# Multi-query attention: the transposes of q, k and the outputs go from TensorE to DMA transposes

## Chip, cores, metric

One core of a Trainium2 chip. The metric is the device time of one execution in microseconds (us). Engines: PE (TensorE: matmuls and transposes), PEld (its weight loads), DVE (VectorE), ACT (ScalarE), POOL (GpSimd), SP (SyncE, which here only issues DMAs). PSUM is the memory into which the code has PE write, SBUF holds all other tiles on the chip.

## The reference

```python
# q: [8, 1024, 16, 64]; k, v: [8, 1024, 64]: all 16 heads share one k and one v
scores = np.matmul(q, k.transpose(0, 1, 3, 2)) / np.sqrt(head_dim)
weights = np.exp(scores - np.max(scores, axis=-1, keepdims=True))
weights = weights / np.sum(weights, axis=-1, keepdims=True)
attn_out = np.matmul(weights, v)
```

## The kernel before

Work goes by *pairs* of heads: 8 batches x 8 pairs = 64. A *window* `w` computes the scores and exponentials of pair `w` while PE sums and multiplies with v for pair `w - 1`. A window has 8 *cycles* (`cy`), each with two *units* of 128x1024 scores. Of a window's 16 units ACT exponentiates 14; units 2 and 8, so in cycles 1 and 4, go to DVE, which does it in seven instructions (`z`, then `f, t, g, t, g, wt`). PE, ACT and DVE run their instructions in the order in which the program emits them.

```python
scp = ctx.enter_context(tc.tile_pool(name="scp", bufs=3, space=PSUM))  # scores: three buffers
b1p = ctx.enter_context(tc.tile_pool(name="b1p", bufs=2, space=PSUM))  # accumulators AND transposes
DVE_UNITS = (2, 8)
# ... (cut)
def trans_q(p):                     # 8 PE transposes, then a DVE copy
    s, r = divmod(p, 2)
    qps = b1p.tile([P, S], FP16, tag="b1", name=f"qps{p}")
    for c in range(NKT):
        nc.tensor.transpose(qps[:, c * P : (c + 1) * P], qn[s][:, c, r * P : (r + 1) * P], ident16)
    qt[p] = qtp.tile([P, S], FP16, tag="qt", name=f"qt{p}")
    nc.vector.tensor_copy(out=qt[p], in_=qps)
# ... (cut)
for w in range(NP + 2):
    a = w - 1
    for cy in range(NCY):
        unit(w, 2 * cy); unit(w, 2 * cy + 1)          # scores, exponential
        for i in range(3 * cy, 3 * cy + 3):
            av_slot(a, i)                             # sums (ones) and products with v
        if cy == 3 and w > 0: trans_q(w + 1)          # 8 transposes + copy
        if cy == 4: sums(a)                           # 4 small transposes + reciprocal
        if cy == 6: finish(a, 0)                      # 4 transposes + multiply
        if cy == 1: finish(w - 2, 1)                  # 4 transposes + multiply + store
        # ... (cut: conditions; k transposed in cycle 7 of the window before a new batch)
        for _ in range(4):
            if late: late.pop(0)()                    # DVE's steps of the exponential
```

The softmax here doesn't subtract the row's maximum and nothing guards it: scores larger than these inputs give would overflow.

## Time and profile before

926.04 us (median of 4 runs, 925.94 to 926.36).

| | before |
|---|---|
| span of the profiled run | 924.2 us |
| ACT busy | 848.8 us (92%) |
| PE busy | 813.3 us (88%) |
| DVE busy | 790.4 us (86%) |
| ACT idle before its exponentials | 62.3 us, 10.7 of it the start |
| pace in steady state | 13.91 us a window |

In the groups of instructions the columns are: line, engine, operation, output<-input tiles and shapes, count | busy us, mean ns of one | idle us of the engine just before them <-what it waited for. Four groups of the kernel before:

```profile
L146 ACT ACTIVATE wt<-sc 128x1024 f16<-128x1024 f32 x896 | 847.5, 1030 | 62.3 <-PE sc L134 54.6
L150 DVE TENSOR_SCALAR z<-sc 128x1024 uint16<-128x1024 f32 x128 | 156.1, 1219 | 60.9 <-PE sc L134 60.9
L222 PE MATMUL tr<-ident,ots 128*128 128x128 f16 x512 | 50.8, 222 | 24.0 <-DVE ots L202 24.0
L123 PE MATMUL qps<-ident,qn 128*128 128x128 f16 x512 | 39.7, 221 | 27.0 <-DVE ots L202 23.2
```

Everybody waits a little: ACT and DVE for PE's scores, PE's transposes for DVE's evictions. Next, ACT alone in order of time in the kernel before (start us, length us, engine, line, operation, shapes, count, idle before and releaser): first three lines from window 0 (the last two of the 13 are window 1's), then lines from steady state.

```profile
12.75 1.94 ACT L146 ACTIVATE wt<-sc 128x1024 f16<-128x1024 f32 x2 [10.73 <-PE sc L134]
15.53 1.02 ACT L146 ACTIVATE wt<-sc 128x1024 f16<-128x1024 f32 x1 [0.84 <-PE sc L134]
17.05 12.02 ACT L146 ACTIVATE wt<-sc 128x1024 f16<-128x1024 f32 x13 [0.49 <-PE sc L134]
...
64.87 11.41 ACT L146 ACTIVATE wt<-sc 128x1024 f16<-128x1024 f32 x12
76.45 1.02 ACT L146 ACTIVATE wt<-sc 128x1024 f16<-128x1024 f32 x1 [0.16 <-PE sc L134]
77.86 12.34 ACT L146 ACTIVATE wt<-sc 128x1024 f16<-128x1024 f32 x13 [0.39 <-PE sc L134]
90.36 1.02 ACT L146 ACTIVATE wt<-sc 128x1024 f16<-128x1024 f32 x1 [0.16 <-PE sc L134]
```

### The profile page before, as it was taken

The numbers are of one execution on the slowest core, as the hardware profiler recorded it, in microseconds if no ns is written. First come the engines' busy times: TensorE is split into PE (matmuls) and PEld (weight loads), VectorE is DVE, ScalarE is ACT, GpSimd is POOL, SyncE is SP. The second block draws the span as 40 slices with busy tenths as digits, with TensorE's granted clock in tenths as the row PEclk, the third lists the DMA queues.
The fourth block names the chain that finished last, engine by engine and source line by source line (L and its number), as shares of the span: only waits on it lengthen the run. The fifth ranks groups of instructions, "written<-read, shape, count | busy, mean of one in ns | idle before, by whom it ended". The sixth has DMA issues, their size and how long they took to land.

```text
span 924.2 us, 18181 instructions
## 1 busy us (share of the span) xinstructions
PE 813.3 (88%) x7488; PEld 291.1 (31%) x7488; DVE 790.4 (86%) x1371; ACT 848.8 (92%) x897; POOL 36.0 (4%) x46
## 2 busy tenths in 40 slices
PE   4998889988898889889899898999898898898986
PEld 1233333333333333333333333333333333333332
DVE  4798898898888898888988988888888889889886
ACT  4999999999999999999999999999999999999994
POOL 3000000000000000000000000000000000000000
PEclk9899999999999999999999999999999999999999
DMA  9033332233232243322342313432314323101102
GB/s 159 4 67 69 58 70 52 47 69 80 49 67 52 47 80 61 61 50 49 76 75 47 69 49 56 75 69 48 65 39 64 70 54 61 47 24 46 47 24 69
DMA packets 116563, 54.64 MB, mean 59 GB/s; under 512 B 18176, under 2 KB 116480, under 8 KB 116480
## 3 DMA queue, kind: packets, MB, share of 16 engines
q0 software_dynamic: 41600, 17.83, 16.3%
q1 hardware_dynamic: 74880, 35.66, 13.7%
q8 instruction: 58, 0.95, 0.4%
q14 instruction: 25, 0.20, 0.1%
HBM read 37.75 MB, written 33.55 MB: 77 GB/s over the span
## 4 chain that ended last, share of the span: by engine, by line
DVE 46%; ACT 27%; PE 20%; issue 6%; DMA 1%; POOL 0%; DVEq 0%; ACTq 0%; POOLq 0%
ACT wt L146 27%; DVE z L150 8%; PE acc L188 6%; PE sc L134 6%; DVE osb L223 5%; DVE ots L202 5%; DVE t L169 5%; DVE wt L175 5%; DVE g L172 5%; PE acc L196 4%; DVE qt L127 4%; DVE t L159 3%; DVE f L156 3%; DVE g L164 3%; PE tr L222 3%
## 5 line engine op out<-in xcount | busy, mean ns | idle before, releaser
L146 ACT ACTIVATE wt<-sc 128x1024 f16<-128x1024 f32 x896 | 847.5, 1030 | 62.3 <-PE sc L134 54.6
L134 PE MATMUL sc<-qt,k2t 64*128 64x512 f16 x2048 | 328.3, 386 | 26.0 <-ACT wt L146 23.0
L196 PE MATMUL acc<-wt,v 128*64 128x512 f16 x2048 | 305.5, 389 | 11.1 <-DVE rec L212 10.9
L150 DVE TENSOR_SCALAR z<-sc 128x1024 uint16<-128x1024 f32 x128 | 156.1, 1219 | 60.9 <-PE sc L134 60.9
L196 PEld LDWEIGHTS <-v 128*64 128x64 f16 x2048 | 90.1, 108 | 199.0 <-issue 172.2
L188 PE MATMUL acc<-wt,ones 128*32 128x512 f16 x2048 | 146.9, 386 | 0.4 <-DVE osb L223 0.3
L134 PEld LDWEIGHTS <-k2t 64*128 64x128 f16 x2048 | 80.9, 94 | 177.3 <-issue 150.4
L202 DVE CAST ots<-acc 128x512 f16<-128x512 f32 x192 | 130.9, 682 | 0.4 <-PE acc L188 0.2
L223 DVE TENSOR_TENSOR osb<-tr,rec 128x512 f32<-128x512 f16 x128 | 88.0, 687 | 36.9 <-PE tr L222 36.0
L175 DVE TENSOR_TENSOR wt<-z,g 128x1024 uint16<-128x1024 uint16 x128 | 88.6, 692 | 13.8 <-ACT wt L146 0.5
L169 DVE TENSOR_TENSOR t<-f,t 128x1024 f16<-128x1024 uint16 x128 | 87.5, 684 | 0.0
L172 DVE TENSOR_TENSOR g<-t,g 128x1024 f16<-128x1024 f16 x128 | 87.1, 680 | 0.1
L222 PE MATMUL tr<-ident,ots 128*128 128x128 f16 x512 | 50.8, 222 | 24.0 <-DVE ots L202 24.0
L123 PE MATMUL qps<-ident,qn 128*128 128x128 f16 x512 | 39.7, 221 | 27.0 <-DVE ots L202 23.2
L188 PEld LDWEIGHTS <-ones 128*32 128x32 f16 x2048 | 37.4, 95 | 73.0 <-issue 58.9
L159 DVE TENSOR_SCALAR t<-f 128x1024 f16<-128x1024 uint16 x128 | 54.7, 427 | 4.4
L112 POOL DMA_DIRECT2D qn<-in_q_dram x32 | 28.2, 882 | 707.4 <-PE qps L123 624.6
L222 PEld LDWEIGHTS <-ots 128*128 128x128 f16 x512 | 28.9, 97 | 81.9 <-DVE ots L202 55.1
L164 DVE TENSOR_SCALAR g<-f 128x1024 f16<-128x1024 uint16 x128 | 53.7, 420 | 0.0
L156 DVE TENSOR_SCALAR f<-z 128x1024 uint16<-128x1024 uint16 x128 | 51.3, 401 | 0.1
L123 PEld LDWEIGHTS <-qn 128*128 128x128 f16 x512 | 34.1, 98 | 51.8 <-issue 47.8
L127 DVE COPY qt<-qps 128x1024 f16<-128x1024 f16 x64 | 43.7, 683 | 5.9 <-PE qps L123 5.9
(18 smaller groups left out, 78.3 us busy)
## 6 DMA issues: line engine op xcount, KB each, us to landing
out_dram<-osb SPq DMA_DIRECT2D x64, 512.0 KB, 3.2
qn<-in_q_dram POOLq DMA_DIRECT2D x32, 512.0 KB, 5.6
kn<-in_k_dram SPq DMA_DIRECT2D x8, 256.0 KB, 3.3
v<-in_v_dram POOLq DMA_DIRECT2D x8, 128.0 KB, 3.5
```

What stands on the lines that cost most here:

```text
L134: nc.tensor.matmul(sc[:, h, :], k2t[64 * h : 64 * h + 64, j * P : (j + 1) * P], qt[p][64 * h : 64 * h + 64, c * QC : (c + 1) * QC], start= ...
L146: nc.scalar.activation(out=w, in_=sc, func=EXP, scale=ascale)
L150: nc.vector.tensor_scalar(out=z, in0=sc, scalar1=15 * ONE, scalar2=None, op0=ALU.add)
L159: nc.vector.tensor_scalar(out=t, in0=f, scalar1=-ONE, scalar2=1.0 / ONE, op0=ALU.add, op1=ALU.mult)
L169: nc.vector.tensor_tensor(out=t, in0=f, in1=t, op=ALU.mult)
L172: nc.vector.tensor_tensor(out=g, in0=t, in1=g, op=ALU.mult)
L175: nc.vector.tensor_tensor(out=w.bitcast(U16), in0=z, in1=g, op=ALU.add)
L188: nc.tensor.matmul(a[32 * g : 32 * g + 32, :], ones16, w[:, h, cq * QC : (cq + 1) * QC], start=(j == 0), stop=(j == NKT - 1), tile_positio ...
L196: nc.tensor.matmul(a[64 * h : 64 * h + 64, :], vt[:, j, :], w[:, h, cq * QC : (cq + 1) * QC], start=(j == 0), stop=(j == NKT - 1), tile_po ...
L202: nc.vector.tensor_copy(out=o, in_=a)
L222: nc.tensor.transpose(tr[:, i, :], ots[p, cq + 1][:, i * P : (i + 1) * P], ident16)
L223: nc.vector.tensor_tensor(out=osb[p][:, 4 * cq : 4 * cq + 4, :].rearrange("p i (h d) -> p (i h) d", h=2), in0=tr.rearrange("p i (h d) -> p ...
```

## The change

The intent: take transposes off PE, the copies behind them off DVE, and both out of the PSUM buffers shared with the accumulators. q, k (from the second batch on) and the outputs with their sums are transposed by DMA, from SBUF to SBUF. The first pair's q and the last pair's output stay on PE.

```diff
     def trans_k(b):
+        if b > 0:
+            st["k2t"] = kvp.tile([P, S], FP16, tag="k2t", name=f"k2t{b}")
+            nc.sync.dma_start_transpose(...)          # cut
+            return
 ...
-        qn[s] = qp.tile([P, NKT, 4 * D], FP16, ...)   # a q load of 4 heads every second window
+        qn[p] = qp.tile([P, NKT, 2 * D], FP16, ...)   # of 2 heads every window
 ...
     def trans_q(p):
+        # cut: p == 0 as before
+        qt[p] = qtp.tile([P, NKT, P], FP16, tag="qt", name=f"qt{p}")
+        nc.sync.dma_start_transpose(out=qt[p], in_=qn[p].rearrange("p c x -> p (c x)"))
 ...
+    def turn(p):
+        otq[p] = otqp.tile([P, 12, P], FP16, tag="otq", name=f"otq{p}")
+        nc.sync.dma_start_transpose(out=otq[p], in_=ots[p].rearrange("p g x -> p (g x)"))
+
+    def finish(p):       # reciprocal and ONE multiply of 128x1024, from SBUF; then the store
 ...
+            load_q(w + 3)
+            trans_q(w + 2)
-                    if cy == 3 and w > 0: trans_q(w + 1)
-                    if cy == 4: sums(a)
-                    if cy == 6: finish(a, 0)
-                if cy == 1 and 0 <= w - 2 < NP: finish(w - 2, 1)
+                    if cy == NCY - 1: turn(a)         # cut: the last pair on PE
+                if cy == 5 and 0 <= w - 2 < NP - 1: finish(w - 2)
```

More of the change, by code (lines that the diff above doesn't have):

```diff
@@ L52 @@
     otsp = ctx.enter_context(tc.tile_pool(name="otsp", bufs=3))
+    otqp = ctx.enter_context(tc.tile_pool(name="otqp", bufs=2))
     recp = ctx.enter_context(tc.tile_pool(name="recp", bufs=3))
@@ L74 @@
     ots: dict = {}
-    rec: dict = {}
-    osb: dict = {}
+    otq: dict = {}
     late: list = []
@@ L96, in trans_k @@
         st = kst[b]
+        if b > 0:
+            st["k2t"] = kvp.tile([P, S], FP16, tag="k2t", name=f"k2t{b}")
+            nc.sync.dma_start_transpose(
+                out=st["k2t"].rearrange("p (c x) -> p c x", x=P),
+                in_=st["k16"].rearrange("p c r d -> p (c r d)"),
+            )
+            return
         kps = b1p.tile([P, S], FP16, tag="b1", name=f"kps{b}")
@@ L105, in trans_k, with load_q @@
         nc.vector.tensor_copy(out=st["k2t"], in_=kps)
-    def load_q(s):
-        if s * 2 >= NP or s in qn:
+    def load_q(p):
+        if p >= NP or p in qn:
             return
-        b, hs = divmod(s, HP // 2)
-        qn[s] = qp.tile([P, NKT, 4 * D], FP16, tag="qn", name=f"qn{s}")
+        b, hp = divmod(p, HP)
+        qn[p] = qp.tile([P, NKT, 2 * D], FP16, tag="qn", name=f"qn{p}")
         nc.gpsimd.dma_start(
-            out=qn[s],
-            in_=q[b, :, 4 * hs : 4 * hs + 4, :].rearrange("(c p) h d -> p c (h d)", p=P),
+            out=qn[p],
+            in_=q[b, :, 2 * hp : 2 * hp + 2, :].rearrange("(c p) h d -> p c (h d)", p=P),
         )
@@ L119, in trans_q @@
             return
-        s, r = divmod(p, 2)
-        qps = b1p.tile([P, S], FP16, tag="b1", name=f"qps{p}")
-        for c in range(NKT):
-            nc.tensor.transpose(
-                qps[:, c * P : (c + 1) * P], qn[s][:, c, r * P : (r + 1) * P], ident16
-            )
-        qt[p] = qtp.tile([P, S], FP16, tag="qt", name=f"qt{p}")
-        nc.vector.tensor_copy(out=qt[p], in_=qps)
+        if p == 0:
+            qps = b1p.tile([P, S], FP16, tag="b1", name="qps0")
+            for c in range(NKT):
+                nc.tensor.transpose(qps[:, c * P : (c + 1) * P], qn[0][:, c, :], ident16)
+            qt[0] = qtp.tile([P, NKT, P], FP16, tag="qt", name="qt0")
+            nc.vector.tensor_copy(out=qt[0].rearrange("p c x -> p (c x)"), in_=qps)
+            return
+        qt[p] = qtp.tile([P, NKT, P], FP16, tag="qt", name=f"qt{p}")
+        nc.sync.dma_start_transpose(
+            out=qt[p], in_=qn[p].rearrange("p c x -> p (c x)")
+        )
     def unit(p, u):
@@ L136, in unit @@
                 k2t[64 * h : 64 * h + 64, j * P : (j + 1) * P],
-                qt[p][64 * h : 64 * h + 64, c * QC : (c + 1) * QC],
+                qt[p].rearrange("p c x -> p (c x)")[
+                    64 * h : 64 * h + 64, c * QC : (c + 1) * QC
+                ],
                 start=True, stop=True, tile_position=(64 * h, 0),
@@ L200, in av_slot, with sums_pe @@
         if j == NKT - 1:
-            o = otsp.tile([P, QC], FP16, tag=f"ots{grp}", name=f"ots{p}_{grp}")
-            nc.vector.tensor_copy(out=o, in_=a)
-            ots[p, grp] = o
-    def sums(p):
+            if grp == 0:
+                ots[p] = otsp.tile([P, 3, QC], FP16, tag="ots", name=f"ots{p}")
+            nc.vector.tensor_copy(out=ots[p][:, grp, :], in_=a)
+    def turn(p):
+        otq[p] = otqp.tile([P, 12, P], FP16, tag="otq", name=f"otq{p}")
+        nc.sync.dma_start_transpose(
+            out=otq[p], in_=ots[p].rearrange("p g x -> p (g x)")
+        )
+    def finish(p):
+        b, hp = divmod(p, HP)
+        o = otq[p]
+        osb = osbp.tile([P, NKT, 2 * D], FP32, tag="osb", name=f"osb{p}")
+        rec = recp.tile([P, NQC, 4, 2], FP32, tag="rec", name=f"rec{p}")
+        nc.vector.reciprocal(
+            out=rec,
+            in_=o[:, 0:4, :].rearrange("p i (c h r) -> p c i h r", c=NQC, h=2)[:, :, :, :, 0],
+        )
+        nc.vector.tensor_tensor(
+            out=osb.rearrange("p i (h d) -> p (i h) d", h=2),
+            in0=o[:, 4:12, :].rearrange("p i (h d) -> p (i h) d", h=2),
+            in1=rec.rearrange("p c i h -> p (c i h)").unsqueeze(2).broadcast_to([P, 16, D]),
+            op=ALU.mult,
+        )
+        nc.sync.dma_start(
+            out=out[b, :, 2 * hp : 2 * hp + 2, :].rearrange("(c p) h d -> p c (h d)", p=P),
+            in_=osb,
+        )
+    def sums_pe(p):
         st = b1p.tile([P, 4, 4], FP32, tag="b1", name=f"st{p}")
@@ L208, in sums, with finish_pe @@
             nc.tensor.matmul(
-                st[:, i, :], ots[p, 0][:, i * P : (i + 1) * P], sel16, start=True, stop=True
+                st[:, i, :], ots[p][:, 0, i * P : (i + 1) * P], sel16, start=True, stop=True
             )
-        rec[p] = recp.tile([P, NQC, 4, 2], FP32, tag="rec", name=f"rec{p}")
-        nc.vector.reciprocal(
-            out=rec[p], in_=st.rearrange("p i (c h) -> p c i h", c=NQC)
-        )
-    def finish(p, cq):
+        rec = recp.tile([P, NQC, 4, 2], FP32, tag="rec", name=f"rec{p}")
+        nc.vector.reciprocal(out=rec, in_=st.rearrange("p i (c h) -> p c i h", c=NQC))
+        end["rec"] = rec
+        end["osb"] = osbp.tile([P, NKT, 2 * D], FP32, tag="osb", name=f"osb{p}")
+    def finish_pe(p, cq):
         b, hp = divmod(p, HP)
-        if cq == 0:
-            osb[p] = osbp.tile([P, NKT, 2 * D], FP32, tag="osb", name=f"osb{p}")
         tr = b1p.tile([P, 4, P], FP16, tag="b1", name=f"tr{p}_{cq}")
         for i in range(4):
-            nc.tensor.transpose(tr[:, i, :], ots[p, cq + 1][:, i * P : (i + 1) * P], ident16)
+            nc.tensor.transpose(
+                tr[:, i, :], ots[p][:, cq + 1, i * P : (i + 1) * P], ident16
+            )
+        half = end["osb"][:, 4 * cq : 4 * cq + 4, :]
         nc.vector.tensor_tensor(
-            out=osb[p][:, 4 * cq : 4 * cq + 4, :].rearrange("p i (h d) -> p (i h) d", h=2),
+            out=half.rearrange("p i (h d) -> p (i h) d", h=2),
             in0=tr.rearrange("p i (h d) -> p (i h) d", h=2),
-            in1=rec[p][:, cq, :, :]
-            .rearrange("p i h -> p (i h)")
-            .unsqueeze(2)
+            in1=end["rec"][:, cq, :, :].rearrange("p i h -> p (i h)").unsqueeze(2)
             .broadcast_to([P, 8, D]),
@@ L231, in finish @@
         )
-        if cq == 1:
-            nc.sync.dma_start(
-                out=out[b, :, 2 * hp : 2 * hp + 2, :].rearrange("(c p) h d -> p c (h d)", p=P),
-                in_=osb.pop(p),
-            )
+        nc.sync.dma_start(
+            out=out[b, 512 * cq : 512 * cq + 512, 2 * hp : 2 * hp + 2, :].rearrange(
+                "(c p) h d -> p c (h d)", p=P
+            ),
+            in_=half,
+        )
+    end: dict = {}
     load_kv(0)
-    load_q(0)
+    for p in range(3):
+        load_q(p)
     cast_k(0)
-    load_q(1)
     with tc.manual_schedule(engines={ENG.PE, ENG.Activation, ENG.DVE}):
@@ L244 @@
         trans_q(0)
+        trans_q(1)
         NCY = NU // 2
@@ L247 @@
             a = w - 1
-            if w % 2 == 0:
-                load_q(w // 2 + 2)
+            load_q(w + 3)
+            trans_q(w + 2)
             if w % HP == 2 and w // HP + 1 < B:
@@ L255 @@
                     unit(w, 2 * cy + 1)
-                if w == 0 and cy == 1:
-                    trans_q(1)
                 if 0 <= a < NP:
@@ L260 @@
                         av_slot(a, i)
-                    if cy == 3 and w > 0:
-                        trans_q(w + 1)
-                    if cy == 4:
-                        sums(a)
-                    if cy == 6:
-                        finish(a, 0)
-                if cy == 1 and 0 <= w - 2 < NP:
-                    finish(w - 2, 1)
+                    if a == NP - 1:
+                        if cy == 3:
+                            sums_pe(a)
+                        if cy == 6:
+                            finish_pe(a, 0)
+                        if cy == 7:
+                            finish_pe(a, 1)
+                    elif cy == NCY - 1:
+                        turn(a)
+                if cy == 5 and 0 <= w - 2 < NP - 1:
+                    finish(w - 2)
                 nb = w // HP + 1
@@ L272 @@
                         cast_k(nb)
-                    if cy == 7:
                         trans_k(nb)
```

## The prediction

> **What bounds it now.** The page's busy table has ACT at 848.8 us (92% of the 924.2 us span), PE 813.3, DVE 790.4. The instructions in order of time show the pace: in steady state one head pair (a window) takes 13.91 us; its 14 exponentials start 0.946 us apart (the groups: 847.5 us / 896), so ACT needs 13.24 us. The rest, about 0.6 us a window, is two or three ACT bubbles (0.16, 0.39, sometimes 0.26 us), each a wait for the score matmul (54.6 us in the list of waits). Each follows PE side work: the eight q transposes, which wait 0.38 us for a VectorE eviction to free their PSUM buffer, and the sum transposes. Seven windows, which also transpose k, take about 14.95 us. First ACT is at 12.75 us (PE waits until 10.29 us for the first q load); about 12.4 us follow the last exponential.
>
> **What the change does.** From PE it takes the q, output, sum and k transposes: 39.7 + 50.8 + 15.4 + 5.3 = 111 us, less the first and last pair, so PE goes to about 704 us; unstalled, that is about 1.31 us per two score units, 10.6 us a window. From DVE go the qt copies (43.7) and most k2t copies (5); two PSUM multiplies of 0.687 us become one of 1024 columns, 1.15 to 1.22 us (estimate from z: 1024 columns, 1.219 us). DVE: about 730 us. Accumulators no longer share buffers with transposes, so PE should hardly wait for VectorE. Added: about 130 crossbar DMA transposes on the SP queue, 256 KB (q) and 384 KB (output) a window, and 32 more q issues on POOL (0.88 us each, off the path).
>
> **Can the transposes keep up?** No trace shows one yet. The Trainium skill, "DMA: Bandwidth & Descriptors", section Latency and other measured facts, has 261 GB/s measured for a DMA transpose; 640 KB are then 2.5 us a window, plus about 2 us fixed each: an estimate of 3 to 4 us per transpose. The output transpose is issued after a window's last eviction and read by DVE five of eight cycles into the next, about 8 us later; q is transposed two windows ahead. Both should be hidden. But "VectorE: DVE Perf Modes", section The three transpose paths, gives 1309 ns for one 128x128 block. If blocks cost that in series, 20 blocks are 26 us a window, twice the window, and the kernel becomes far slower. I take that figure as mostly latency.
>
> **On the critical path:** nearly all the gain is ACT's bubbles: 57 x about 0.6 plus 7 x about 1.6 = 45 us, of which I expect four fifths (36); the shorter first q load gives 3 to 5 us; the tail about 1 us. 926 - 41 = 885.
>
> **Prediction: 885 us, 80% range 872 to 918.** Faster by over 2%: 0.77; within 2%: 0.10; slower by over 2%: 0.13.
>
> **What would show it.** ACT's busy time unchanged at about 848 us, 95 to 96% of the span; window period 13.25 to 13.5 us; ACT's wait for the score matmul under 20 us; no extra time at batch boundaries; PE near 704, DVE near 730; the output transpose under 8 us from issue to landing; DVE's reciprocal hardly waiting on DMA; first ACT at about 10 us.
>
> **What would make it wrong.** A transpose of 8 us or more, or SP kept busy issuing descriptors, so that the reciprocal on DVE waits, then z, the score buffers and ACT; transpose traffic beyond the window; transposes slowing the q loads or output DMAs; bubbles that came from DVE's late z rather than PE's transposes, which would stay.

## More of the kernel before

*Ballast* is useless work, added to see whether its time shows.

Last, a stretch of the chain of waits of the kernel before (start us, length us, what), just before an ACT bubble:

```profile
42.86 0.39 PE sc L134 x2
43.25 0.76 PE acc L188 x12
44.01 0.34 PE tr L222 x4
44.35 0.02 issue
44.38 0.69 DVE osb L223
45.07 0.34 DVE f L156
...
48.03 0.69 DVE wt L175
48.72 0.60 DVE qt L127
49.33 1.13 DVE z L150
50.46 0.17 DVE rec L212
50.63 0.04 issue
50.67 0.62 PE acc L196 x4
51.29 0.34 PE sc L134 x2
51.63 0.03 ACTq L146
51.66 0.32 ACT wt L146
```

It goes from PE (scores, sums, the output transposes of cycle 1) into DVE, stays there 6 us without a pause, then back to PE, which may not go on with the accumulation before DVE has read the sums (`rec`), and so to ACT. No engine is full; this stretch suggests that a loop through three engines sets the pace, which the experiments test. Over the whole span the page of the kernel before divides this chain so:

```profile
DVE 46%; ACT 27%; PE 20%; issue 6%; DMA 1%; POOL 0%; DVEq 0%; ACTq 0%; POOLq 0%
```

## The result

847.5 us (median of 8 runs, 846.82 to 848.13), against 925.94 (13 runs). The ratio is 0.9154, 95% interval 0.9145 to 0.9163: faster by 8.5%. (A ratio is the mean time of one kernel's fast runs over that of the other's in the same rounds, so not quite the ratio of the medians.) The prediction's direction was right; the time lies below its range, by 24.5 us.

| | before | after |
|---|---|---|
| span | 924.2 | 845.6 us |
| ACT busy | 848.8 (92%) | 823.3 (97%) |
| PE busy | 813.3 | 739.6 |
| DVE busy | 790.4 | 759.6 |
| first exponential | 12.75 | 10.42 us |
| pace in steady state | 13.91 | 12.84 us a window |
| share of the DMA engines, two main queues | 30% | 72% |

The groups after that answer to those of before:

```profile
L159 ACT ACTIVATE wt<-sc 128x1024 f16<-128x1024 f32 x896 | 822.0, 1138 | 10.3 <-PE sc L145 10.1
L163 DVE TENSOR_SCALAR z<-sc 128x1024 uint16<-128x1024 f32 x128 | 156.2, 1220 | 48.2 <-PE sc L145 47.6
L229 DVE RECIPROCAL rec<-otq 128x16 f32<-128x16 f16 x63 | 15.2, 242 | 0.3 <-DMA otq<-ots 0.3
```

The same 896 exponentials of the same shape have 25.5 us less busy time. Their mean length went *up*, from 1030 to 1138 ns, which fits with more of them starting while the one ahead is still running. ACT after, in order of time:

```profile
10.42 1.94 ACT L159 ACTIVATE wt<-sc 128x1024 f16<-128x1024 f32 x2 [8.40 <-PE sc L145]
...
99.50 734.82 ACT L159 ACTIVATE wt<-sc 128x1024 f16<-128x1024 f32 x801
```

From 99.50 us on there are 801 exponentials without a gap that the view shows, to the last one, on average (734.82 - 1.02) / 800 = 0.917 us apart: the average that the kernel before reached in window 0 alone. 14 of them make 12.84 us, which is the new pace. Single starts are again 0.904 us apart; only two of a window (units 4 and 10) still wait for their scores, by under 0.1 us and without a gap. The whole difference of the two spans can be read from ACT's row:

| where | before | after | gain |
|---|---|---|---|
| bubbles after the first exponential (idle less the start) | 62.3 - 10.7 = 51.6 | 10.3 - 8.4 = 1.9 | 49.7 us |
| waits hidden in the overlap (exponentials' busy time) | 847.5 | 822.0 | 25.5 us |
| until the first exponential | 12.75 | 10.42 | 2.3 us |
| after the last one | 12.5 | 11.2 | 1.2 us |
| sum | | | 78.7 us, to rounding 924.2 - 845.6 |

Counted from single starts, the 25.5 us are not waits that left no gap at all; those cost 10.7 us in both kernels. They are the overlapped first parts of waits that did leave a gap: 26.7 us in 197 waits before, 1.0 us in five after.

The chain after, over about as long, is PE and ACT alone:

```profile
77.76 0.39 PE sc L145 x2
78.15 0.76 PE acc L201 x12
78.91 0.54 PE sc L145 x4
79.45 0.55 PE acc L201 x8
80.00 0.34 PE acc L209 x2
80.33 0.34 PE sc L145 x2
80.67 0.03 ACTq L159
80.70 1.60 ACT wt L159 x2
```

The DMA transposes, from the list of DMA issues after (output<-input, queue, operation, count, median us from issue to landing):

```profile
qt<-qn SPq DMA_TRANSPOSE x63, 4.3
otq<-ots SPq DMA_TRANSPOSE x63, 4.3
```

### The profile page after: what moved, and what is told of

Its sections match the earlier page's. It is cut to its first block, busy times and chain, and to the rows that moved or that the text cites. A ratio compares the mean times of both kernels' runs of the same rounds, so it can differ in the third digit from the quotient of the medians.

```text
span 845.6 us, 15710 instructions
## 1 busy us (share of the span) xinstructions
PE 739.6 (87%) x6172; PEld 225.8 (27%) x6172; DVE 759.6 (90%) x1238; ACT 823.3 (97%) x897; POOL 64.4 (8%) x78
## 4 chain that ended last, share of the span: by engine, by line
ACT 51%; PE 40%; DVE 5%; issue 2%; DMA 1%; ACTq 0%; POOL 0%; POOLq 0%; DVEq 0%
ACT wt L159 51%; PE sc L145 18%; PE acc L209 12%; PE acc L201 10%; DVE z L163 2%; DMA qn<-in_q_dram 1%; DMA otq<-ots 0%; DVE ots L216 0%; DVE t L182 0%; DVE f L169 0%; DVE wt L188 0%; ACTq L159 0%; DVE g L185 0%; DVE t L172 0%; DVE g L177 0%
## 5 line engine op out<-in xcount | busy, mean ns | idle before, releaser
L159 ACT ACTIVATE wt<-sc 128x1024 f16<-128x1024 f32 x896 | 822.0, 1138 | 10.3 <-PE sc L145 10.1
L145 PE MATMUL sc<-qt,k2t 64*128 64x512 f16 x2048 | 370.2, 387 | 93.0 <-ACT wt L159 90.4
L209 PE MATMUL acc<-wt,v 128*64 128x512 f16 x2048 | 293.6, 388 | 0.0
L145 PEld LDWEIGHTS <-k2t 64*128 64x128 f16 x2048 | 97.9, 93 | 399.6 <-issue 390.6
L120 POOL DMA_DIRECT2D qn<-in_q_dram x64 | 56.6, 884 | 647.8 <-DMA qt<-qn 634.0
L233 DVE TENSOR_TENSOR osb<-otq,rec 128x1024 f32<-128x1024 f16 x63 | 77.2, 1225 | 2.1
L169 DVE TENSOR_SCALAR f<-z 128x1024 uint16<-128x1024 uint16 x128 | 56.1, 438 | 4.4
L229 DVE RECIPROCAL rec<-otq 128x16 f32<-128x16 f16 x63 | 15.2, 242 | 0.3 <-DMA otq<-ots 0.3
L85 POOL DMA_DIRECT2D v<-in_v_dram x8 | 7.2, 894 | 36.1 <-PE acc L209 35.7
L91 DVE TENSOR_SCALAR k<-kn 128x512 f16<-128x512 f32 x16 | 6.1, 423 | 3.2 <-DMA kn<-in_k_dram 3.2
```

Of the source, the lines that this page charges most:

```text
L120: nc.gpsimd.dma_start(out=qn[p], in_=q[b, :, 2 * hp : 2 * hp + 2, :].rearrange("(c p) h d -> p c (h d)", p=P),)
L145: nc.tensor.matmul(sc[:, h, :], k2t[64 * h : 64 * h + 64, j * P : (j + 1) * P], qt[p].rearrange("p c x -> p (c x)")[64 * h : 64 * h + 64, ...
L159: nc.scalar.activation(out=w, in_=sc, func=EXP, scale=ascale)
L169: nc.vector.tensor_scalar(out=f, in0=z, scalar1=1023, scalar2=None, op0=ALU.bitwise_and)
L209: nc.tensor.matmul(a[64 * h : 64 * h + 64, :], vt[:, j, :], w[:, h, cq * QC : (cq + 1) * QC], start=(j == 0), stop=(j == NKT - 1), tile_po ...
L233: nc.vector.tensor_tensor(out=osb.rearrange("p i (h d) -> p (i h) d", h=2), in0=o[:, 4:12, :].rearrange("p i (h d) -> p (i h) d", h=2), in ...
```

## The experiments

Two questions. Is 0.917 us really ACT's own pace, so that ACT was waiting even while it looked busy? And what held it back: PE's time for transposes (theory P), PE's waiting for DVE at them (W), or DVE's load (V)? Sixteen kernels ran, each with a run of the kernel before on the same chip in three rounds (925.8 to 926.2 us). "After" is the changed kernel at 847.5 us.

### ACT ballast on both kernels

```diff
+                if w < NP and cy == 3:
+                    nc.scalar.activation(out=bal2, in_=bal, func=EXP, scale=ascale)   # 128x256, result unused
```

> The changed kernel plus one useless 128x256 exponential on ACT a window, about 0.28 us each, 18 us in all. If the changed kernel is bound by ACT's own service time (12.84 us a window), the time rises by all of it: 863 to 867 us. If something else bounds it, by less.

> The kernel before, with the same 0.28 us ACT ballast a window. If its ACT needed 13.24 us of 13.91 with 0.6 us of bubbles, as predicted, most of the 18 us shows, 935 to 944 us. If its ACT was waiting 1.07 us a window (bubbles plus waits hidden between overlapping exponentials), the ballast is largely absorbed: 926 to 933 us.

In the trace the ballast puts the next start 0.306 us later, 19.6 us in all. After: 866.05 us (ratio to before 0.9351, 0.9337 to 0.9365), 18.6 us more: 0.29 us a window, nearly all of it. The changed kernel is bound by ACT's own pace, but for the two short waits a window. Before: 922.7 us (0.9958, 0.994 to 0.9975): the same work cost nothing; it even ran 0.4% faster, which no run here explains. So the kernel before was not bound by ACT, although its busy share was the highest.

### Putting parts back on PE

`a_q_on_pe`: q transposes and copy back in cycle 3 of the window before. `b_out_on_pe`: sums and outputs back in cycles 4, 6 and 1. `f_k_on_pe`: k back in cycle 7. Core of the three edits to the changed kernel:

```diff
-            trans_q(w + 2)                       # a: DMA
+                    if cy == 3 and w > 0:
+                        trans_q(w + 1)           # a: 8 PE transposes and a DVE copy
-                    elif cy == NCY - 1:
-                        turn(a)                  # b: DMA; finish(w - 2) in cycle 5 goes too
+                    if cy == 4: sums_pe(a)
+                    if cy == 6: finish_pe(a, 0)
+                if cy == 1 and 0 <= w - 2 < NP: finish_pe(w - 2, 1)
+                    if cy == 7: trans_k(nb)      # f: 8 PE transposes and a DVE copy
```

> The changed kernel with only the q transposes put back on PE (with their PSUM buffer and the 0.68 us copy on VectorE); outputs and k stay on the DMA. Theory W (ACT was starved because PE, in order, waits at transposes for VectorE evictions and for shared PSUM buffers): one of three waiting sites returns, so part of the 78 us does, some 20 to 30 us: 868 to 878 us. Theory P (PE time): 8 of 20 transposes, 40 us of PE's 111, return: about 28 us if it is proportional, but nearly nothing if PE's slack of 1.4 us a window absorbs it. Theory V (VectorE load): 0.68 us a window more on VectorE, 12.5 of 12.84 us: small, under 10 us.

> The changed kernel with only the output and sum transposes put back on PE; q and k stay on the DMA. Theory W: two waiting sites (the transposes behind the evictions, the accumulator behind the reciprocal) return, the larger part: 880 to 900 us. Theory P: 12 of 20 transposes, 66 of 111 us of PE time: about 45 us, 890 us. Theory V: VectorE gains only 0.15 us a window: stays at about 850 us.

> The changed kernel with the k transposes on PE, in cycle 7 of the window before, as in the old kernel. The old kernel's seven batch windows took about 1 us more than the others. Expected: that cost returns, 3 to 8 us: 850 to 855 us; if the slack of PE hides it, 848.

Measured: q 848.95 us (+1.4), outputs 883.09 (+35.6), k 851.77 (+4.3). The 1.4 us are within the noise. Singly they give 41 us; all together, which is the kernel before (whose q loads are different too), 78. The parts do not add up: the transposes use up a slack that one of them alone does not exhaust. And q's eight transposes with their copy cost almost nothing, though they are 40 of the 111 us of PE's transposes and DVE is then busier (793.9 us) than in the kernel before (790.4). Plain theory P and plain theory V both fall here.

### PE's time alone, waiting alone, DVE's load alone

`c_pe_ballast`: 20 useless matmuls a window in the accumulator before its first matmul clears it. `d_wait_only`: tiny matmuls at the old places that read what the transposes read. `e_dve_ballast`: one more DVE instruction.

```diff
+        if j == 0:                                               # c, in av_slot
+            for _ in range((4, 8, 8)[grp]):
+                nc.tensor.matmul(a[:, 0:P], ident16, ident16, start=True, stop=True)
+    def poke(p, grp):                                            # d, in cycles 3, 4, 6 and 1
+        lhs = ident16 if grp is None else ots[p][:, grp, 0:P]
+        t = b1p.tile([P, 4, 4], FP32, tag="b1", name=f"poke{p}_{grp}")
+        for i in range(4 if grp == 0 else 1):
+            nc.tensor.matmul(t[:, i, :], lhs, sel16, start=True, stop=True)
+        # cut: for grp == 0 a reciprocal on DVE reads t
+                    if cy == 3:                                  # e
+                        nc.vector.tensor_tensor(out=bal2, in0=bal, in1=bal, op=ALU.mult)  # 128x1024 f16
```

> The changed kernel plus 20 useless 128x128 matmuls a window (4, 8 and 8), written into the accumulator tile just before its own first matmul clears it: the PE time of the removed transposes returns, with no new PSUM buffer, no VectorE work and no new wait. Theory W: PE has about 2 us of slack a window and the time is hidden or nearly so: 847 to 856 us. Theory P: most of the gain is lost: 890 us or more.

> The changed kernel plus tiny matmuls (128x4; one at three sites, four at the sum site) at the four places where the old kernel transposed, each in a tile of the shared PSUM pool, three of them reading the eviction just made; VectorE reads only the sum tile (0.25 us). It returns the waits without the PE time (under 0.5 us a window) and with 0.25 us of VectorE work. Theory W: much of the 78 us returns: 875 to 915 us. Theories P and V: under 855 us.

> The changed kernel plus one useless 128x1024 f16 multiply on VectorE a window (about 0.68 us, busy 12.55 of 12.84 us, a little more than the old kernel's 12.35). Theory V (the gain came from relieving VectorE): a large part is lost, 880 us or more. Theory W: still below the window, so under 855 us.

Measured: PE's time 880.16 us (+32.7), waiting 853.97 (+6.5), DVE 848.4 (+0.9, with DVE busy 800.7 us, again more than before the change). Theory W, which I favoured, falls as a cause on its own: waiting alone is worth 6.5 us. (Both DVE additions, the copy of q and this one, stand in cycle 3; no other cycle was tried.) PE's time counts, here in cycles 0, 2 and 5, yet in the run with q on PE eight transposes were free. The difference that is left is the *place*: theory P2.

### The place

Theory P2: in cycles 1 and 4 one of two units goes to DVE, so ACT gets one tile of scores for the cycle's whole PE work; PE time added there comes straight between ACT and its next scores. `m_pe_time_old_places` puts useless matmuls at the places of all the old transposes, with no DVE work behind them; `q_pe_time_cy1` puts eight in cycle 1 alone.

```diff
+    def poke(p, cy, n, cols):
+        t = b1p.tile([P, P], FP32, tag="b1", name=f"poke{p}_{cy}")
+        for i in range(n):
+            nc.tensor.matmul(t[:, 0:cols], ident16, ident16[:, 0:cols], start=True, stop=True)
+        PLACES = {1: (4, P), 3: (8, P), 4: (4, 4), 6: (4, P)}    # m
+        PLACES = {1: (8, P)}                                     # q
```

> The changed kernel with useless matmuls of the size and at the places of all the old transposes (4 in cycle 1, 8 in cycle 3, four small ones in cycle 4, 4 in cycle 6), in a tile of the shared PSUM pool that nobody reads: the old PE program without VectorE work and with hardly a wait for VectorE. Theory P2 (PE time costs where it falls after a unit that goes to VectorE: there ACT gets one tile of scores and PE has no slack; in cycle 3 it is free): as with the outputs alone on PE, 875 to 890 us. Theory P (all PE time counts): 910 us or more. Theory W: under 860 us.

> The changed kernel with 8 useless matmuls a window, as many as the q transposes, in cycle 1 only. The q transposes in cycle 3, with their copy and waits, cost 1.4 us. Theory P2: in cycle 1 the same PE time, about 0.55 to 0.62 us, shows in full: 876 to 888 us. If the place does not matter: under 855 us.

Measured: eight in cycle 1 877.24 us (0.9471, 0.9456 to 0.9485), +29.7: 0.47 us a window of the 0.55 us that they take. The same number of transposes in cycle 3, with a copy and a PSUM buffer on top, had cost 1.4 us. That shows the place. All old places together: 874.25 us, +26.7.

The traces show where the slack is. In the changed kernel PE waits for ACT to free a score buffer before units 1, 3, 9 and 15 of a window (cycles 0, 1, 4 and 7), 0.35, 0.36, 0.35 and 0.30 us (means of windows 6 to 59). With q's transposes in cycle 3 the waits before 9 and 15 are gone and 0.32 us before unit 11 has come. With eight matmuls in cycle 1 all four stand, and ACT waits instead. In `c_pe_ballast` those before 3, 9 and 15 are down to 0.03, 0 and 0, and the time still rises, since its 20 matmuls take 1.37 us a window (at 0.55 us for eight). Read so, PE time is free where a wait of PE follows in time to absorb it, and only up to that wait's length; P2's cycles 1 and 4 are not the only ones that cost.

The chain of waits of the run with eight in cycle 1 is that of after with one line more:

```profile
67.42 0.39 PE sc L145 x2
67.81 0.76 PE acc L201 x12
68.57 0.55 PE poke L280 x8
69.12 0.54 PE sc L145 x4
69.66 0.55 PE acc L201 x8
70.21 0.34 PE acc L209 x2
70.54 0.34 PE sc L145 x2
70.89 0.03 ACTq L159
70.91 1.50 ACT wt L159 x2
```

It takes 3.49 us from the first line to ACT's start (70.91 - 67.42), against 2.94 us after (80.70 - 77.76). ACT works off three tiles in 3 x 0.917 = 2.75 us and there are three score buffers; that this number of buffers is what sets the limit is argued, not shown: no run had a fourth.

### What is left: DVE in the loop

PE's time at the old places explains 27 of the 78 us, outputs on PE 36. `n_before_dve_light` takes one of six steps (0.68 us, twice a window) out of DVE's exponential in the kernel before, `o_out_on_pe_dve_light` does so in the kernel with outputs on PE. Both compute a wrong exponential.

```diff
         def s4():
-            nc.vector.tensor_tensor(out=t, in0=f, in1=t, op=ALU.mult)
+            pass
```

> The kernel before without one of the six steps of the exponential on VectorE (0.68 us, twice a window; the result is wrong on purpose). Its chain of waits runs through VectorE without a pause for 6 us a window. If that chain holds it at 926 (theory L: the combination closes a loop through VectorE), it falls to what PE's placed work alone allows, 880 to 895 us. If VectorE does not matter: over 915 us.

> The kernel with only outputs and sums on PE (883 us), without the same step on VectorE (wrong result on purpose). Its chain shows PE and ACT, not VectorE. Theory P2: VectorE does not matter here: 878 to 884 us. If VectorE mattered: under 865 us.

Before: 882.0 us (0.9521, 0.9507 to 0.9535), 44 us less, and DVE's part of its chain of waits falls from 46% to 9% (the chain's shares by engine, this run):

```profile
ACT 45%; PE 36%; issue 9%; DVE 9%; DMA 1%; ACTq 0%; POOL 0%; DVEq 0%; POOLq 0%
```

So in the kernel before DVE's work did hold the time, while more DVE work than that is free in the changed kernel (`e_dve_ballast`, `a_q_on_pe`, both in cycle 3). Among the runs that add or take DVE work, it mattered only where outputs and sums are on PE. The time shows this, not the share of the chain: `e_dve_ballast`, only 0.9 us slower than the changed kernel, has a chain that runs mostly through DVE:

```profile
DVE 73%; ACT 14%; PE 8%; issue 4%; DMA 1%; DVEq 0%; POOL 0%; ACTq 0%; POOLq 0%
```

The second run, 868.84 us, missed its expectation of 878 to 884: 14 of the 36 us of the outputs on PE go through DVE too, though the stretch of that kernel's chain that I had looked at shows none (over the whole span it is 12%).

### Would other places have done?

`r_out_on_pe_moved` keeps outputs on PE but in cycles 3, 6 and 7; `s_before_moved` is the kernel before with all its transposes at other cycles.

```diff
-                    if cy == 4: sums_pe(a)                 # s: sums(a)
-                    if cy == 6: finish_pe(a, 0)            # s: finish(a, 0)
-                if cy == 1 and ...: finish_pe(w - 2, 1)    # s: finish(w - 2, 1)
+                    if cy == 6: sums_pe(a)
+                    if cy == 7: finish_pe(a, 0)
+                if cy == 3 and ...: finish_pe(w - 2, 1)
-                    if cy == 3 and w > 0: trans_q(w + 1)   # s only
+                    if cy == 2 and w > 0: trans_q(w + 1)
```

> The kernel with outputs and sums on PE (883 us), but the transposes moved out of cycles 1, 4 and 6 into cycles 3, 6 and 7. If only the place mattered (theory P2 alone): 850 to 862 us, most of the 35 us comes back without any DMA transpose of outputs. If PE time and round trips count wherever they stand: 875 to 890 us.

> The kernel before, with q transposes in cycle 2 instead of 3, sums in 6 instead of 4, output halves in 7 and 3 instead of 6 and 1; no DMA transposes. If places and the loop through VectorE that they close explain the 78 us: 860 to 890 us. If the work itself must go: 915 us or more.

Measured: 870.39 us and 956.62 us (1.0333, 1.0317 to 1.0348). The first gets 13 of its 35.6 us back and falls between the two expectations; the second is 3% *slower* than the kernel before. Both chains now run mostly through DVE (67% and 57%, against 46% before); in the second, q transposes wait 72.5 us for DVE's evictions, against 23.2 before. From its list of waits (who waited for whom, us in total, times, longest):

```profile
PE qps L123 <- DVE ots L202: 72.5, 62, 1.2
```

Leaving the old cycles is not enough. My reading of these waits, which no run tests: transposes on PE read what DVE has just evicted and hold a buffer that DVE must free, so a new place closes another loop. Neither choice of places reaches the 847.5 us of the change; whether a good one exists is open.

### How much room the DMA transposes have

`g_out_turned_twice` transposes each output a second time into a tile that nobody reads. `h_finish_cy1` has DVE read the transposed output in cycle 1 instead of 5.

```diff
+        spare = otqp.tile([P, 12, P], FP16, tag="spare", name=f"spare{p}")               # g
+        nc.sync.dma_start_transpose(out=spare, in_=ots[p].rearrange("p g x -> p (g x)"))
-                if cy == 5 and 0 <= w - 2 < NP - 1:                                      # h
+                if cy == 1 and 0 <= w - 2 < NP - 1:
```

> The changed kernel with each output transposed twice, the second time into a tile nobody reads: 384 KB more a window. The DMA engines' share is about 72% in the changed kernel; this adds some 20 points. If the transposes are hidden with room to spare: 847 to 851 us. If the queue is nearly full: 860 us or more, with VectorE's reciprocal waiting for the DMA.

> The changed kernel with the output's normalisation on VectorE in cycle 1 instead of cycle 5 of the next window. The transpose lands about 4.3 us after its issue; in cycle 1 VectorE would get there after about 1.5 to 2 us and wait 2 to 3 us a window, more than its slack of about 0.97 us: the window grows by 1.5 to 2 us, 920 to 975 us. If the transpose were already there: 848 us.

Twice: 848.67 us (+1.2) with the two main queues' share of the DMA engines at 91% instead of 72%. Throughput has room. Early: 1053.9 us (1.1376, 1.1327 to 1.1426), worse than expected: DVE waits 4 us a window, and PE another 149.9 us in all for DVE to evict accumulators. First the group, then two lines in order of time (the issue on SP and DVE's reciprocal):

```profile
L229 DVE RECIPROCAL rec<-otq 128x16 f32<-128x16 f16 x63 | 16.0, 254 | 249.1 <-DMA otq<-ots 249.1
312.98 1.42 SPq L220 DMA_TRANSPOSE otq<-ots  x1
318.40 0.25 DVE L229 RECIPROCAL rec<-otq 128x16 f32<-128x16 f16 x1 [4.31 <-DMA otq<-ots]
```

From the issue to DVE's start it takes 5.4 us here (318.40 - 312.98). In the changed kernel DVE asks 8.8 us after the issue (77.20 and 86.03 us in one window) and waited in one of 63 cases, for 0.3 us. Without the late `finish` the change would have been a loss. (PE's granted clock was 0.907 in this profiled run and 0.913 to 0.926 in the other three, against 0.999 after; how much of the loss goes with the clock is not separated.)

## Why the prediction was right or wrong

- **Direction, and the transposes being hidden: right.** 4.3 us from issue to landing (predicted 3 to 4, limit 8), DVE's reciprocal waited 0.3 us in all, and the output transposed twice changed nothing. The bad case, blocks in series at the 1309 ns that the Trainium skill, "VectorE: DVE Perf Modes", The three transpose paths, gives for one of 128x128, did not come: 12 blocks landed in 4.3 us.
- **The step that failed: "its 14 exponentials start 0.946 us apart ... so ACT needs 13.24 us."** 0.946 is busy time over count, not ACT's need: it contains waits hidden in the overlap. The changed kernel's ACT takes 0.917 us, 12.84 us a window (predicted 13.25 to 13.5), and starts that wait for nothing are 0.904 us apart in both kernels. The ballast runs bear it out: nearly all of it shows after, none before. This term was left out of the sum and measured 25.5 us. It could have been read beforehand from 13 exponentials in 12.02 us in window 0. One formula of the Trainium skill makes the same error look right: "ScalarE: Activation LUTs", What ACT_TABLE_LOAD costs, gives 186 ns + 0.833 ns a column (scale and bias immediate) and an overlap of about 93 ns, which makes an estimate of 946 ns for 1024 columns; the trace says 904.
- **The discount.** "I expect four fifths (36)" of 45 us of bubbles. There were 51.6, and 49.7 went. With 25.5 from the term above, this makes 75.2 in place of 36; start and tail gave 3.5 of the predicted 4 to 6.
- **"Each follows PE side work": right in outline, wrong in detail.** I named the q transposes and the sums; q alone in its old place costs 1.4 us. What costs is PE time where PE has no wait left to absorb it (shown: 29.7 us for eight matmuls in cycle 1), k (4.3 us), and DVE's work, once transposes on PE wait for it (shown: 44 us less from lightening DVE in the kernel before; which transposes close that loop is not). How the 37 us that no part alone accounts for (78 less 41, up to 3.5 of them start and tail) divide among the loops is not settled.
- **"ACT's busy time unchanged", "PE near 704, DVE near 730": wrong**, 823.3, 739.6 and 759.6. On PE and DVE too, neighbouring instructions overlap: PE's groups before add up to more (328.3 + 305.5 + 146.9 + 50.8 + 39.7 + 15.4 + 5.3 = 891.9 us) than its busy time (813.3), and so do DVE's (870 against 790.4). Taking a group's time off the busy time takes off overlap as well.
- **"No extra time at batch boundaries", first exponential at about 10 us, ACT's wait for scores under 20 us: right.** ACT's visible waits for scores are 10.1 us in all, 8.4 of them the start; k back on PE costs 4.3 us for seven boundaries.

## What to carry to other kernels

Busy time over count is not an engine's need: read the spacing of starts where the inputs are surely early, and if the mean lies above it, the busy time holds waits that no gap shows; a small ballast on the supposed bottleneck tests this in one run. When three engines hand work round in order and none is full, the cost of an instruction depends on where in the order it stands (does a wait of its engine follow that can absorb it?) and what it makes others wait for, so parts tested singly need not add up. A DMA transpose takes a step out of such a loop, if its consumer is placed later than its latency, read from issue to use.

## What the Trainium skill lacked or had wrong

- "ScalarE: Activation LUTs", What ACT_TABLE_LOAD costs: its formula with its overlap gives, as an estimate, 946 ns between starts of a 128x1024 exponential; here, from PSUM scores, it was 904 ns (917 on average of 801, waits included), one alone 1.02 us.
- "Perfetto Trace Analysis", Identifying the Most-Contended Engine, calls the engine of highest occupancy the most contended, and occupancy a fair measure of how close ScalarE is to roofline. Here ACT had the highest, 92%, of which 25.5 us were hidden waits that the change removed, and 19.6 us of added ACT work cost that kernel nothing.
- "DMA: Bandwidth & Descriptors", Latency and other measured facts: 261 GB/s for a DMA transpose, measured on one kernel with a non-contiguous middle dimension. This case stays below it by an estimate from the queue's share of the 16 engines in the runs with and without the second output transpose: (0.679 x 847.5 - 0.487 x 845.6) / 63 = 2.6 us of all engines for 384 KB (393,216 bytes), 151 GB/s; issue to landing 4.3 us.
- "VectorE: DVE Perf Modes", The three transpose paths, has 1309 ns for one block by DMA and does not say how that grows with blocks. Here 8 and 12 blocks both landed in a median of 4.3 us.
